# The beginning of a diffusion-layer kernel: more single-tile blocks, products ahead of the modulation matvecs, and another order of loads

## The chip, the cores and the metric

The kernel runs on one core of a Trainium2 chip. The time is the device time of one execution in microseconds; lower is better. Before the change three runs took 2594.56, 2595.95 and 2599.84 us, so the median is 2595.95 us. The execution that was profiled took 2596.07 us.

The engines are named as the profile names them: PE (matrix products; PEld its weight loads), DVE (vector), ACT (scalar and activation), POOL, and SP, which here only issues DMAs. Each engine runs its own instructions in the order of the program and waits on semaphores for the others.

## The reference, cut to what matters

One layer of a hybrid backbone. Only its first step is touched by the change: the modulation vectors of the first FFN, and the beginning of that FFN's first product.

```python
silu_c = jax.nn.silu(c)                  # latent tokens; silu_cc for context tokens
mod_l = (silu_c @ w_mod[l] + b_mod[l]).reshape(B, N_MOD, D_MODEL)    # w_mod: 2048 x 9*2048

def adaln(x, g, mod, i):
    return rms_norm(x, g) * (1 + mod[:, i + 1, None, :]) + mod[:, i, None, :]

def half_step_ffn(x, mod, i, g, w_up, w_down):
    h = adaln(x, g, mod, i)
    a, b = jnp.split(h @ w_up, 2, axis=-1)
    return x + 0.5 * mod[:, i + 2, None, :] * ((jax.nn.silu(a) * b) @ w_down)
```

There are 256 context and 256 latent tokens, the model width is 2048, and all inputs are float32.

## The kernel before, in words

**What the beginning does.** The 2048 columns of the model are 16 tiles of 128 (k = 0 to 15). For each tile k the kernel needs the modulation's shift (i = 0) and scale (i = 1) of these 128 columns for both conditions, before it can form h for that tile; and it can multiply the tile's h by the weights as soon as that is there. So it does not compute all the modulation first. It goes through the columns in `BLOCKS`: two blocks of one tile, (0, 1) and (1, 2), then seven blocks of two tiles.

**One block.** `mod_sums` multiplies the conditions by a 2048 x (block's columns) piece of `w_mod`: 16 small matrix products (32 rows out) per 1 MB load. These are called matvecs here, and the loads are numbered 0 to 31 in the order in which SP issues them (tile `mraw`, four buffers). `mod_turned` copies nothing but turns the sums' rows into columns (PE transposes of `row`) and DVE adds them up to SH (shift) and SC (scale). Then PE turns the tile's columns of x (transposes of `xs`), ACT and DVE form h from them, as a high part `hhi` and a low part `hlo` (`affine_split`: two ACT passes for `hhi`, one pass on ACT and one on DVE for h, one on DVE for `hlo`, for each 256 tokens of a two-tile block).

A block of one tile takes two loads, one for the shift and one for the scale, both by PE. A block of two tiles takes four loads: the first holds the shift of the block's first tile and is summed by DVE in two long passes over 128 x 2048 (`scalar_tensor_tensor`, one for each condition, `junkv<-mraw,cB`); the other three are matvecs of PE. So load 4 was DVE's in block (2, 4), load 8 in (4, 6), load 12 in (6, 8).

**Products.** `products` loads the weights of the first six output units for a block (`w_pre1`, tile `raw`: 384 KB for one tile, 768 KB for two), splits them into `hi` (ACT) and `lo` (DVE), and multiplies: per unit and tile hi by hhi, lo by hhi, and hi by hlo, 128 x 512 each, into six PSUM banks that stay open for all 16 tiles. It is a generator: one step issues the load, the next the split, each further step one unit's products. While a block's matvecs run, PE is given the products of the block before: after each matvec `3 - (k1 - k0)` units, the rest around the block's transposes.

**What sets the order.** Nearly everything in the beginning is pinned: PE, DVE, ACT and SP run it in the order of the Python code. SP issues each load when its buffer has been read by whoever read it last, and in turn: a load that waits holds back all behind it. The four `mraw` buffers go round, so a load of the next block waits for PE's matvec or for DVE's second long pass over a load of this block. After the beginning (about 130 us) comes the rest of the layer, whose code is untouched.

Of the kernel before, what the change touches and what calls it, by code (L numbers as in the profile page):

```python
# [9 lines left out]
F32 = mybir.dt.float32  # L10
F32R = mybir.dt.float32r
BF16 = mybir.dt.bfloat16
FP8 = mybir.dt.float8e5
AF = mybir.ActivationFunctionType
ALU = mybir.AluOpType
# [15 lines left out]

WAIT = 3

N_IDLE = 6, 4, 5, 2, 3

N_HID = 3

# [4 lines left out]

BLOCKS2 = tuple((k, k + 4) for k in range(0, 16, 4))

BLOCKS = ((0, 1), (1, 2)) + tuple((k, k + 2) for k in range(2, 16, 2))
FB = 4
CB = 512
NCB = D // CB
# [10 lines left out]
def tile_layer(ctx: ExitStack, tc: tile.TileContext, I: dict, out: bass.AP):  # L59
# [16 lines left out]
    def tbank():  # L76
        return ps["tr"].tile([P, 512], F32, tag="tr", name="tr")
# [189 lines left out]
    class Beside:  # L267
# [139 lines left out]
    def products(n_ffn, pre, k0, k1, hhi, hlo, early=False, both=False, middle=False):  # L407

        n = (k1 - k0) * P
        most = min(2 * NPRE, 2048 // n // 2 * 2)

        def load(u0):
            nu = min(most, 2 * NPRE - u0)
            raw = raw_tile(n * nu)

            o = (2 * NPRE * k0 * P + u0 * n) * P  # L420
            tc.keep_in_program_order(nc.sync.dma_start(raw, I[f"w_pre{n_ffn}"][o : o + n * nu * P].rearrange("(p c) -> p c", p=P)))
            return raw, nu

        ahead = [load(0)]
        if early:
            wt = split(ahead[0][0], n * ahead[0][1])
        if both:
            ahead.append(load(most))
        yield
        if middle:  # L430
            wt = split(ahead[0][0], n * ahead[0][1])
            early = True
            yield
        for u0 in range(0, 2 * NPRE, most):
            raw, nu = ahead.pop(0)
            if u0 or not early:
                wt = split(raw, n * nu)
            if u0 + most < 2 * NPRE and not ahead:
                ahead.append(load(u0 + most))
            for u in range(nu):  # L440
                b = pre[(u0 + u) // 2][u % 2]
                ws = [(k, wt(slice(u * n + (k - k0) * P, u * n + (k - k0 + 1) * P))) for k in range(k0, k1)]

                for k, (wh, wl) in ws:
                    tensor[0].matmul(b, wh, hhi[:, k, :], start=k == 0, stop=False)  # L445
                    tensor[0].matmul(b, wl, hhi[:, k, :], start=False, stop=False)  # L446
                for k, (wh, wl) in ws:
                    tensor[0].matmul(b, wh, hlo[:, k, :], start=False, stop=k == KT - 1)  # L448
                yield

    xsrc = {CTX: I["ctx"], LAT: I["x"]}
# [10 lines left out]
    with pool(name="st", bufs=1) as st:  # L462
        scratch.append(st)
        cP = st.tile([P, KT, 32], F32, name="cP")
        nc.gpsimd.memset(cP, 0.0)
        pc = tbank()
        nc.tensor.transpose(pc[:, :32], cc, ident[:32, :32])
        nc.vector.tensor_copy(cP[:, :, 0:2], pc[:, :32].rearrange("p (s k) -> p k s", s=2))
# [4 lines left out]

        cB = st.tile([P, 2, D], F32, name="cB")
        junk = st.tile([P, 1024], BF16, name="junkv")
        sel = st.tile([96, P], BF16, name="sel")[:, :32]
        with nc.allow_low_precision("each sum has one term that is not zero, and that is one"):
            vector[0].tensor_reduce(sel, ident[:96, :96].rearrange("p (j q) -> p q j", j=3), axis=AX.X, op=ALU.add)
        c3 = tbank()[:96, :P]
        stack = st.tile([32, P], F32, name="stack")  # L480
        vector[0].tensor_copy(stack[:, :96].rearrange("p (j q) -> p j q", j=3), ident[:32, :32].unsqueeze(1).to_broadcast([32, 3, 32]))
        tensor[0].matmul(c3, stack[:, :96], cc, start=True, stop=True)
        thirds = st.tile([96, P], BF16, name="thirds")
        middle = st.tile([96, P], BF16, name="middle")
# [68 lines left out]
        def mod_unit():  # L553
            if ready:
                return ready.pop(0)
            raw = st.tile([P, 2048], F32, tag="mraw", name="mraw", bufs=4)
            tc.keep_in_program_order(nc.sync.dma_start(raw, I["w_m0"][next(unit)]))
            return raw

        def mod_sums(i, k0, k1, last=iter(())):  # L560

            n = (k1 - k0) * P
            nk = 2048 // n
            b = tbank()[:, :n]
            for g in range(KT // nk):
                if g == KT // nk - 1:
                    steps(last)
                raw = mod_unit()
                for j in range(nk):
                    k = nk * g + j  # L570
                    q = 32 * (j % 4)
                    tensor[0].matmul(
                        b[q : q + 32, :], cP[:, k, :], raw[:, j * n : (j + 1) * n], start=k < 4, stop=k >= KT - 4, tile_position=(0, q), skip_group_check=True
                    )
                yield
            row = st.tile([P, 256], F32, tag="row", name="row", bufs=3)[:, :n]
            scalar[0].activation(row, b, AF.Copy)
            turns.append((i, k0, k1, row))
# [28 lines left out]
        def idle(n):  # L607

            for _ in range(n):
                tensor[0].matmul(pre[2][0][:, :P], ident, ident, start=True, stop=True, skip_group_check=True)  # L610
# [23 lines left out]
        others(1, True)  # L634
        drain(mod_sums(1, 0, 1))
        mod_turned()
        for s in (CTX, LAT):
            scale_of(0, s, slice(0, 1))
        steps(prods)
# [9 lines left out]
        for k0, k1 in BLOCKS[1:]:  # L649
            kk = slice(k0, k1)  # L650
            following = products(1, pre, k0, k1, hhi, hlo, middle=True)
            if k1 - k0 == 2:
                raw = mod_unit()
            for i in range(2):
                for _ in mod_sums(i, k0 if i else k1 - 1, k1, following if i else iter(())):
                    steps(prods, 3 - (k1 - k0))
                if not i and k1 - k0 == 2:
                    for s in (CTX, LAT):
                        vector[0].scalar_tensor_tensor(
                            junk.bitcast(FP8), raw, 1.0, cB[:, s, :], op0=ALU.mult, op1=ALU.mult, accum_out=SH[:, 0, s, k0 : k0 + 1], saturate=False  # L660
                        )
                    biased(0, k0, k0 + 1)

            if k0 != 2:
                steps(following)
            mod_turned()
            if k0 != 2:
                steps(prods)
            for s in (CTX, LAT):
                scale_of(0, s, kk)  # L670
            if k0 == 2:
                steps(following)
                steps(prods)
            if k1 - k0 == 1:
                tb = tbank()
                for s in (CTX, LAT):
                    for t in range(2):
                        x_turned(k0, s, t, tb)
                x_scaled(k0, tb)
            else:  # L680
                for s in (CTX, LAT):
                    drain(to_hT([xs0[s, 0], xs0[s, 1]], 0, s, hhi, hlo, 256 * s, range(k0, k1)))
            drain(prods)
            prods = following
            if k0 == 2:
                scalar[0] = nc.scalar
            if k1 == KT:
                nc.sync.dma_start(ccd.rearrange("s (k p) -> (s k) p", p=P), cc)
# [1770 lines left out]
```

## Time and profile before

| what | value |
|---|---|
| median of three runs | 2595.95 us |
| profiled execution | 2596.07 us, its span 2594.4 us |
| PE busy | 2565.9 us, 99% of the span |
| DVE, ACT, POOL busy | 2183.9, 1432.4, 220.5 us |
| PE busy in the first 130 us | 116.3 us |
| DMA in the first 130 us | 374 GB/s, engines 94% busy |

Where the profile's page counts PE as busy, a row of the timeline gives start, duration, engine, line of the source, operation, the names out<-in, the count, and in brackets the idle time before and what ended it. All pinned instructions of the beginning carry the line of one helper, L87 in the kernel before and L90 in the changed one, so the names tell them apart. A matvec of 16 is counted there as 32 (two passes each).

### The profile page before, as it was taken

Reading aid. Unit: us, or ns where it says so; the run is one execution under the profiler, and the core shown is the slowest. Engines: PE = TensorE matmul, PEld = TensorE weight load, DVE = VectorE, ACT = ScalarE, POOL = GpSimd, SP = SyncE. Lnnn points to the kernel's source line nnn. Section 1 sums busy time; section 2 is a strip of 40 time slices with the busy share of each in tenths; the row PEclk is TensorE's granted clock in tenths of the full one; section 3 lists DMA queues with packets and bytes.
Section 4 is the critical chain, followed back from the end, with each engine's and each line's share of the span. In section 5 each row is a group of like instructions: output and inputs, shape, how many; then the busy total and the mean of one; then the engine's idle time right before and its main releaser. Section 6 shows DMA issues by size and latency. Waiting matters only on the chain. (4 is left out here: it accounts for less than half of the span.)

```text
span 2594.4 us, 34281 instructions
## 1 busy us (share of the span) xinstructions
PE 2565.9 (99%) x12708; PEld 2141.1 (83%) x12708; DVE 2183.9 (84%) x2884; ACT 1432.4 (55%) x1838; POOL 220.5 (8%) x273
## 2 busy tenths in 40 slices
PE   7999999999999999999999999999999999999998
PEld 5788888888888888888889989888898888888887
DVE  6788888878888788888887899798889888888987
ACT  4454444544445565444454448456486676667764
POOL 0000000100000100000110000120000000001001
PEclk9999999999999999999999999999999999999999
DMA  9989999999999989889987897776768999999986
GB/s 396 353 215 266 267 287 273 259 275 287 257 291 264 279 245 244 213 220 224 230 255 258 294 328 239 239 282 212 261 229 251 274 275 277 283 280 284 272 247 174
DMA packets 127656, 684.73 MB, mean 264 GB/s; under 512 B 14200, under 2 KB 16760, under 8 KB 64896
## 3 DMA queue, kind: packets, MB, share of 16 engines
q1 hardware_dynamic: 98112, 490.63, 50.6%
q0 software_dynamic: 29376, 191.90, 37.5%
q8 instruction: 100, 1.64, 0.2%
q14 instruction: 68, 0.56, 0.1%
HBM read 664.59 MB, written 17.89 MB: 263 GB/s over the span
## 5 line engine op out<-in xcount | busy, mean ns | idle before, releaser
L128 ACT ACTIVATE hi<-raw 128x1024 fp32r<-128x1024 f32 (+2 forms) x488 | 505.6, 1040 | 412.6 <-PE mm L152 304.4
L129 DVE TENSOR_TENSOR lo<-raw,hi 128x1024 fp32r<-128x1024 f32 (+2 forms) x476 | 569.0, 1204 | 134.0 <-ACT hi L128 113.2
L128 ACT ACTIVATE hi<-chain 128x1024 fp32r<-128x1024 f32 x352 | 371.9, 1060 | 305.9 <-PE mm L152 184.4
L129 DVE TENSOR_TENSOR lo<-chain,hi 128x1024 fp32r<-128x1024 f32 x352 | 426.5, 1221 | 105.8 <-ACT hi L128 98.3
L152 PE MATMUL mm<-hi,hhi 128*128 128x512 f32 (+3 forms) x1024 | 394.0, 385 | 0.0
L152 PE MATMUL mm<-lo,hhi 128*128 128x512 f32 (+3 forms) x1024 | 386.9, 378 | 0.0
L152 PE MATMUL mm<-hi,hlo 128*128 128x512 f32 (+3 forms) x1024 | 386.4, 377 | 0.0
L208 DVE SCALAR_TENSOR_TENSOR junk<-sraw,cBh 128x1024 fp8e5<-128x1024 f32 x192 | 234.3, 1220 | 21.4 <-DMA sraw<-in_w_mt 19.0
L152 PEld LDWEIGHTS mm<-lo,hhi 128*128 128x128 f32 x1024 | 192.5, 188 | 33.8
L152 PEld LDWEIGHTS mm<-hi,hhi 128*128 128x128 f32 x1024 | 192.6, 188 | 31.1
L152 PEld LDWEIGHTS mm<-hi,hlo 128*128 128x128 f32 x1024 | 192.8, 188 | 30.7
L129 DVE TENSOR_TENSOR lo<-ra,hi 128x1024 fp32r<-128x1024 f32 x104 | 126.3, 1221 | 27.4 <-ACT hi L128 21.6
L128 ACT ACTIVATE hi<-ra 128x1024 fp32r<-128x1024 f32 x104 | 110.2, 1062 | 66.4 <-PE mm L152 40.5
L152 PE MATMUL mm<-lo,hid2h 128*128 128x512 f32 (+1 forms) x356 | 137.9, 387 | 0.1
L152 PE MATMUL mm<-hi,hid2h 128*128 128x512 f32 (+1 forms) x356 | 137.8, 387 | 0.0
L152 PE MATMUL mm<-hi,hid2l 128*128 128x512 f32 (+1 forms) x356 | 137.7, 387 | 0.0
L152 PE MATMUL mm<-hi,sumshl 128*128 128x512 f32 x400 | 123.2, 389 | 0.0
L730 POOL DMA_DIRECT2D chain<-in_w_up1b x60 | 53.1, 886 | 733.5 <-DVE lo L129 733.5
L208 DVE SCALAR_TENSOR_TENSOR sr<-sr,cBl 128x1024 f32<-128x1024 f32 x84 | 102.2, 1224 | 13.4 <-DMA sr<-in_w_mt 7.4
L152 PE MATMUL mm<-hi,sumshh 128*128 128x512 f32 x352 | 108.4, 389 | 0.0
L152 PE MATMUL mm<-hhi,hi 128*128 128x512 f32 (+1 forms) x288 | 101.3, 352 | 0.0
L152 PE MATMUL mm<-hhi,lo 128*128 128x512 f32 (+1 forms) x288 | 99.0, 344 | 0.0
(505 smaller groups left out, 5446.4 us busy)
## 6 DMA issues: line engine op xcount, KB each, us to landing
raw<-in_w_dn SPq DMA_DIRECT2D x70, 1024.0 KB, 9.7
chain<-in_w_up1b POOLq DMA_DIRECT2D x60, 1024.0 KB, 10.6
sraw<-in_w_mt SPq DMA_DIRECT2D x96, 512.0 KB, 8.1
sr<-in_w_mt SPq DMA_DIRECT2D x81, 512.0 KB, 5.6
raw<-in_w_up1b SPq DMA_DIRECT2D x40, 1024.0 KB, 8.0
mraw<-in_w_m SPq DMA_DIRECT2D x32, 1024.0 KB, 8.0
chain<-in_w_dn POOLq DMA_DIRECT2D x30, 1024.0 KB, 9.2
chain<-in_w_up2b POOLq DMA_DIRECT2D x28, 1024.0 KB, 11.2
```

The source lines that it names most:

```text
L128: scalar[0].activation(hi, src, AF.Copy)
L129: vector[0].tensor_tensor(lo, src, hi.bitcast(F32), op=ALU.subtract)
L152: tensor[0].matmul(out_ap, s, m, start=first and not n, stop=last and n == 2, skip_group_check=skip)
L208: ins = nc.vector.scalar_tensor_tensor(junk() if junk else raw, raw, 1.0, cB[s], op0=ALU.mult, op1=ALU.mult, accum_out=mT[:, i, s, kt, h : ...
L730: accum = lambda dst, src: nc.gpsimd.dma_start(dst, src, accum_op=ALU.add)
```

## The change

Five edits, all in the beginning:

- Tiles 2 and 3 become blocks of one tile each (`ALONE = 4`). Loads 4 to 7 are now all summed by PE; DVE's first long passes are those of load 8.
- `AHEAD` says for blocks 1 to 4 how many units of the products of the block before stand ahead of the first matvec and behind each matvec; `idle(N_IDLE[5])` adds four 128 x 128 products that nobody reads behind tile 0's transposes.
- In blocks of one tile the low part's product of a unit stands behind the next unit's high parts ("one unit on").
- Up to block (4, 6) the load of a block's weights is issued behind its last modulation load, where it was issued ahead of it.
- `stack` and `sel`, two small constants, are made by DVE ahead of the copy of the turned conditions.

From block (6, 8) on, and through the whole rest of the layer, every engine has the same instructions in the same order as before, but for the buffers.

PE, from the transposes of tile 0's sums to the first products. Before (`tr<-mraw,cP` is a matvec, `mm<-hhi,hi`, `mm<-hhi,lo` and `mm<-hlo,hi` are a unit's three products):

```order
L87 MATMUL tr<-ident,row 128x128 x2
L87 MATMUL tr<-mraw,cP 32x128 x16
L87 MATMUL mm<-hhi,hi 128x512
L87 MATMUL mm<-hhi,lo 128x512
L87 MATMUL mm<-hlo,hi 128x512
L87 MATMUL mm<-hhi,hi 128x512
```

And now:

```order
L90 MATMUL tr<-ident,row 128x128 x2
L90 MATMUL mm<-ident 128x128 x4
L90 MATMUL mm<-hhi,hi 128x512
L90 MATMUL mm<-hhi,lo 128x512
L90 MATMUL mm<-hhi,hi 128x512
L90 MATMUL mm<-hhi,lo 128x512
L90 MATMUL mm<-hlo,hi 128x512
L90 MATMUL tr<-mraw,cP 32x128 x16
```

The matvec of load 2 has moved behind four idle products and five products of tile 0, and the first product with hlo stands fifth instead of third.

DVE, from tile 1's hlo to the first long passes. Before:

```order
L87 TENSOR_SCALAR h<-tr,SC,SH 128x256
L87 TENSOR_TENSOR hlo<-h,hhi 128x512
L87 SCALAR_TENSOR_TENSOR junkv,SH<-mraw,cB 128x2048 x2
L87 TENSOR_TENSOR SH<-SH,vecs 128x2
L87 TENSOR_REDUCE SH<-tr 128x2
```

And now, where tile 3's hlo is the one ahead of them:

```order
L90 TENSOR_SCALAR h<-tr,SC,SH 128x256
L90 TENSOR_TENSOR hlo<-h,hhi 128x512
L90 SCALAR_TENSOR_TENSOR junkv,SH<-mraw,cB 128x2048 x2
L90 TENSOR_TENSOR SH<-SH,vecs 128x2
L90 TENSOR_REDUCE SH<-tr 128x2
```

The long passes over load 4 are gone, and those over load 8 are the first; they stand behind tile 3's h and hlo (before: behind those of the block of tiles 2 and 3).

SP, the loads 8 to 15, with the engines whose semaphores each waits for (the number in a name only counts the tiles; DMAHW is an earlier load of SP). Before, the rows are loads 9, 10, weights, 11, 12, 13, 14, weights, 15:

```order
L557 DMA mraw_536<-in_w_m0 128x2048 [waits DMAHW6_49,DMAHW2_49,PE_49]
L557 DMA mraw_566<-in_w_m0 128x2048 [waits DMAHW4_49,DVE_49]
L421 DMA raw_582<-in_w_pre1 128x1536 [waits Activation_49]
L557 DMA mraw_584<-in_w_m0 128x2048 [waits DMAHW0_49,PE_49]
L557 DMA mraw_661<-in_w_m0 128x2048 [waits DMAHW2_49,PE_49]
L557 DMA mraw_664<-in_w_m0 128x2048 [waits DMAHW7_49,DMAHW3_49,PE_49]
L557 DMA mraw_694<-in_w_m0 128x2048 [waits DMAHW1_49,DVE_49]
L421 DMA raw_710<-in_w_pre1 128x1536 [waits Activation_49]
L557 DMA mraw_712<-in_w_m0 128x2048 [waits DMAHW5_49,PE_49]
```

And now loads 9, 10, 11, weights, 12, 13, 14, weights, 15:

```order
L563 DMA mraw_614<-in_w_m0 128x2048 [waits DMAHW5_49,DMAHW3_49,PE_49]
L563 DMA mraw_644<-in_w_m0 128x2048 [waits DMAHW7_49,PE_49]
L563 DMA mraw_660<-in_w_m0 128x2048 [waits DMAHW0_49,PE_49]
L424 DMA raw_662<-in_w_pre1 128x1536 [waits DMAHW6_49,DVE_49]
L563 DMA mraw_719<-in_w_m0 128x2048 [waits DMAHW3_49,PE_49]
L563 DMA mraw_722<-in_w_m0 128x2048 [waits DMAHW2_49,DVE_49]
L563 DMA mraw_752<-in_w_m0 128x2048 [waits DMAHW4_49,DMAHW1_49,PE_49]
L424 DMA raw_768<-in_w_pre1 128x1536 [waits Activation_49]
L563 DMA mraw_770<-in_w_m0 128x2048 [waits DMAHW5_49,PE_49]
```

The load that waits for DVE (for the second long pass over load 8) was load 14 and is now load 13, and load 13 is the one whose matvec PE reaches first in block (6, 8).

```diff
-N_IDLE = 6, 4, 5, 2, 3
+N_IDLE = 6, 4, 5, 2, 3, 4
+
+AHEAD = {1: (2, 2, 1), 2: (0, 1, 2), 3: (0, 1, 2), 4: (1, 2, 2, 1)}
...
-BLOCKS = ((0, 1), (1, 2)) + tuple((k, k + 2) for k in range(2, 16, 2))
+ALONE = 4
+BLOCKS = tuple((k, k + 1) for k in range(ALONE)) + tuple((k, k + 2) for k in range(ALONE, 16, 2))
...
+            behind = []
             for u in range(nu):
...
-                for k, (wh, wl) in ws:
-                    tensor[0].matmul(b, wh, hlo[:, k, :], start=False, stop=k == KT - 1)
+                behind += [(b, k, wh) for k, (wh, wl) in ws]
+                while behind and (k1 - k0 > 1 or u == nu - 1 or len(behind) > 1):
+                    o, k, wh = behind.pop(0)
+                    tensor[0].matmul(o, wh, hlo[:, k, :], start=False, stop=k == KT - 1)
                 yield
...
-                if g == KT // nk - 1:
+                if g == KT // nk - 1 and k1 > ALONE + 2:
                     steps(last)
                 raw = mod_unit()
+                if g == KT // nk - 1 and k1 <= ALONE + 2:
+                    steps(last)
...
         mod_turned()
+        idle(N_IDLE[5])
...
+            ahead = iter(AHEAD.get(k0, ()))
+            steps(prods, next(ahead, 0))
             for i in range(2):
                 for _ in mod_sums(i, k0 if i else k1 - 1, k1, following if i else iter(())):
-                    steps(prods, 3 - (k1 - k0))
+                    steps(prods, next(ahead, 3 - (k1 - k0)))
...
-            if k0 != 2:
+            if k0 != ALONE:
                 steps(following)
             mod_turned()
-            if k0 != 2:
+            if k0 != ALONE:
                 steps(prods)
             for s in (CTX, LAT):
                 scale_of(0, s, kk)
-            if k0 == 2:
+            if k0 == ALONE:
                 steps(following)
                 steps(prods)
```

More of the change, by code (lines that the diff above doesn't have):

```diff
@@ L465, in tile_layer @@
         nc.gpsimd.memset(cP, 0.0)
+        stack = st.tile([32, P], F32, name="stack")
+        pin(nc.vector.tensor_copy(stack[:, :96].rearrange("p (j q) -> p j q", j=3), ident[:32, :32].unsqueeze(1).to_broadcast([32, 3, 32])))
+        sel = st.tile([96, P], BF16, name="sel")[:, :32]
+        with nc.allow_low_precision("each sum has one term that is not zero, and that is one"):
+            pin(nc.vector.tensor_reduce(sel, ident[:96, :96].rearrange("p (j q) -> p q j", j=3), axis=AX.X, op=ALU.add))
         pc = tbank()
@@ L475, in tile_layer @@
         junk = st.tile([P, 1024], BF16, name="junkv")
-        sel = st.tile([96, P], BF16, name="sel")[:, :32]
-        with nc.allow_low_precision("each sum has one term that is not zero, and that is one"):
-            vector[0].tensor_reduce(sel, ident[:96, :96].rearrange("p (j q) -> p q j", j=3), axis=AX.X, op=ALU.add)
         c3 = tbank()[:96, :P]
-        stack = st.tile([32, P], F32, name="stack")
-        vector[0].tensor_copy(stack[:, :96].rearrange("p (j q) -> p j q", j=3), ident[:32, :32].unsqueeze(1).to_broadcast([32, 3, 32]))
         tensor[0].matmul(c3, stack[:, :96], cc, start=True, stop=True)
@@ L684, in tile_layer @@
             prods = following
-            if k0 == 2:
+            if k0 == ALONE:
                 scalar[0] = nc.scalar
```

## The prediction

> **What bounds the kernel now.** I read the page's busy shares first, then the stretches of the beginning, then PE's timeline there with the waits in brackets, then the other engines and SP's loads at those waits.
>
> ```profile
> span 2594.4 us, 34281 instructions
> PE 2565.9 (99%) x12708; PEld 2141.1 (83%) x12708; DVE 2183.9 (84%) x2884; ACT 1432.4 (55%) x1838; POOL 220.5 (8%) x273
> ```
>
> PE is the bound. The stretches (length, then busy time of PE, PEld, DVE, ACT, POOL, then the granted clock, DMA share and GB/s) tell where it isn't busy:
>
> ```profile
> 0.00:20.64 20.64, 13.70 (x145) 11.79 (x145) 11.93 (x40) 13.52 (x31) 4.18 (x13) 1.00 0.91 365
> 20.64:58.78 38.14, 31.54 (x292) 21.55 (x293) 24.06 (x51) 16.52 (x33) 0.00 (x0) 0.96 1.01 420
> 58.78:71.93 13.15, 13.15 (x113) 9.29 (x112) 9.70 (x18) 4.98 (x10) 0.00 (x0) 1.00 0.97 369
> 71.93:85.08 13.15, 13.15 (x113) 9.29 (x113) 9.71 (x18) 4.97 (x10) 0.00 (x0) 1.00 0.95 353
> 130.00:2594.40 2464.40, 2449.64 (x11695) 2056.97 (x11693) 2092.77 (x2702) 1373.57 (x1722) 216.27 (x260) 1.00 0.88 258
> ```
>
> From 20.64 (tile 0's sums turned) to 58.78 (first matvec of block (6, 8)) PE idles 38.14 - 31.54 = 6.6 us while the DMA engines are full. From 58.78 on each two-tile block takes PE 13.15 us without a gap. So the end moves by what the arrival in block (6, 8) moves, as long as PE then finds its data; 6.6 us, with the slow clock below about 8, is the most that is there to gain. PE's waits and prices:
>
> ```profile
> 23.61 1.08 PE L87 MATMUL tr<-mraw,cP 128*32 128x128 f32 x32 [2.98 <-DMA mraw<-in_w_m]
> 24.62 0.78 PE L87 MATMUL mm<-hhi,hi 128*128 128x512 f32 x1
> 27.46 1.36 PE L87 MATMUL tr<-mraw,cP 128*32 128x128 f32 x32
> 28.75 0.49 PE L87 MATMUL mm<-hhi,hi 128*128 128x512 f32 x1
> 31.15 0.60 PE L87 MATMUL tr<-ident,xs 128*128 128x128 f32 x4
> 34.63 0.51 PE L87 MATMUL mm<-hlo,hi 128*128 128x512 f32 x1 [0.51 <-DVE hlo L87]
> 38.58 1.07 PE L87 MATMUL tr<-mraw,cP 128*32 128x256 f32 x16 [1.54 <-DMA mraw<-in_w_m]
> 50.83 1.07 PE L87 MATMUL tr<-mraw,cP 128*32 128x256 f32 x16 [1.25 <-DMA mraw<-in_w_m]
> 55.06 1.04 PE L87 MATMUL tr<-ident,xs 128*128 128x128 f32 x8
> 55.86 0.48 PE L87 MATMUL mm<-hhi,hi 128*128 128x512 f32 x1
> 58.78 1.08 PE L87 MATMUL tr<-mraw,cP 128*32 128x128 f32 x32
> 59.79 0.50 PE L87 MATMUL mm<-hhi,hi 128*128 128x512 f32 x1
> 60.13 0.40 PE L87 MATMUL mm<-hhi,lo 128*128 128x512 f32 x1
> 60.36 0.39 PE L87 MATMUL mm<-hhi,hi 128*128 128x512 f32 x1
> 63.98 1.07 PE L87 MATMUL tr<-mraw,cP 128*32 128x256 f32 x16
> ```
>
> Read by starts: a matvec costs 1.01 (58.78 to 59.79), the first product behind it 0.34, each further one 0.23, eight transposes of x 0.80. Matvec and six products after 23.61 run slowly: 24.62 to 27.46 is 2.84 us for 1.5 at these prices, and the matvec of load 3 takes 1.29. That is 1.6 us lost.
>
> **The change, part by part.**
>
> *Products ahead, low part one unit on, idle products.* These fill PE's waits. The first products of tile 0 can start when hhi is there, the first with hlo when DVE has made it:
>
> ```profile
> 21.27 1.02 ACT L87 ACTIVATE hhi<-mm,SH,SC 128x256 fp32r<-128x256 f32 x2 [0.19 <-DVE SC L87]
> 23.36 0.69 DVE L87 TENSOR_TENSOR hlo<-h,hhi 128x512 fp32r<-128x512 f32 x1
> ```
>
> So from 22.3 PE does four products, waits until 24.05 for hlo, then goes on with load 2 (there by 23.61). The four idle products cost nothing: they lie in the wait up to 22.3, and without that cover would cost 0.5. What is late next is hlo, 0.7 us of wait, and at tile 1 the same chain, for which I allow 0.6.
>
> *Two blocks of one tile.* One matvec more on PE (four for tiles 2 and 3 where three were): 1.0 us, on the path. Two turned rows' transposes instead of three per pair become four: 0.1. DVE loses two long passes of 2.3 us and gets a second set of sums. The bytes loaded are the same. Tile 2's products no longer wait for loads 6 and 7, which is what frees PE to run ahead.
>
> *Weights behind the modulation load, earlier constants.* Load 3 comes one 384 KB load sooner (0.9 us at 420 GB/s), its weights one 1 MB load later (2.5 us); their split on ACT stands behind the copy of load 3's sums anyway, so I cost this at nothing, with load 3's matvec as cover; if that cover were gone it would cost up to 2.5. The constants move c's spreading by up to 0.6 us, but x's last load hides all but 0.1 to 0.2 of it.
>
> *The sum up to block (6, 8).* PE's work between 20.64 and 58.78 at full clock is 31.54 - 1.6 = 29.9. With 1.0 + 0.5 + 0.1 more it is 31.5; the waits left are 22.3 - 20.64 less the 0.7 of idle products, 0.7 and 0.6, together 2.2 to 2.3. PE reaches the end of block (4, 6) at 20.64 + 31.5 + 2.2 = 54.3, where before it was 58.78: 4.5 us ahead.
>
> *The wait that is added.* Ahead of that stands load 13. Its buffer is now the one of load 8, which DVE reads twice, and SP holds loads 14, 15 and the block's weights behind it. Before, load 13 waited for a matvec of PE and went out at 48.05; it was load 14 that waited for DVE. The long passes before and SP's loads, each with the time from issue to landing:
>
> ```profile
> 46.12 2.28 DVE L87 SCALAR_TENSOR_TENSOR junkv<-mraw,cB 128x2048 fp8e5<-128x2048 f32 x1
> 48.45 2.29 DVE L87 SCALAR_TENSOR_TENSOR junkv<-mraw,cB 128x2048 fp8e5<-128x2048 f32 x1
> 59.16 0.69 DVE L87 TENSOR_TENSOR hlo<-h,hhi 128x512 fp32r<-128x512 f32 x1
> 48.05 0.33 SPq L557 DMA_DIRECT2D mraw<-in_w_m  x1
> mraw<-in_w_m SPq DMA_DIRECT2D x1, 1024.0 KB, 7.6
> 51.96 0.33 SPq L557 DMA_DIRECT2D mraw<-in_w_m  x1
> mraw<-in_w_m SPq DMA_DIRECT2D x1, 1024.0 KB, 10.4
> 59.92 0.33 SPq L557 DMA_DIRECT2D mraw<-in_w_m  x1
> mraw<-in_w_m SPq DMA_DIRECT2D x1, 1024.0 KB, 6.2
> 73.07 0.33 SPq L557 DMA_DIRECT2D mraw<-in_w_m  x1
> mraw<-in_w_m SPq DMA_DIRECT2D x1, 1024.0 KB, 7.7
> 118.96 0.33 SPq L900 DMA_DIRECT2D raw<-in_w_up1b  x1
> raw<-in_w_up1b SPq DMA_DIRECT2D x1, 1024.0 KB, 4.8
> ```
>
> When do the passes over load 8 end now? Going back from 54.3: tile 3's transposes end ahead of block (4, 6)'s three matvecs (3.0), 18 products (4.2, and 0.5 for first ones), transposes (0.25 and 0.8), and the seven products of tile 2 (1.7), so at about 43.7. In the trace x's transposes for tile 1 began at 31.15 and hlo let the product go at 34.63, so hlo follows the transposes' end by about 2.8: 46.5. Two passes take 4.6 (46.12 to 50.74): load 13 goes out at 51.1, 3 us later than before. At that time only load 12 is ahead of it on the queue, so it does not stand in a stream any more. Its landing is bounded by 4.8 us (118.96, an empty queue) and 7.7 (73.07); I take 6.2, the load at 59.92, which also went out with one load ahead of it. That is 57.3. Load 15 landed 6.7 us behind load 13 before (48.05 + 7.6 and 51.96 + 10.4): now 64.0. Its matvec began at 63.98.
>
> The Trainium skill (DMA: Bandwidth & Descriptors, Anatomy of one DMA) puts a DMA's fixed part at about 2.0 us beside its bytes, which with 1 MB at 436 GB/s is an estimate of 4.4 us: load 13 at 55.5 and load 15 at 62.2. The rows above, 6.2 and 7.7 behind one other load, speak for more.
>
> So the 4.5 us of lead are waited away ahead of loads 13 to 15, and PE goes on from load 15's matvec where it was. With 4.8 instead of 6.2 load 15 lands 1.4 sooner, with 7.7 it lands 1.5 later. I take 6.2, and 0.2 for the earlier constants: the profiled execution's 2596.07 (0.12 above the median) becomes 2595.9.
>
> *The clock.* PE's busy time in three windows of 3.4 us, with the granted clock behind it (the second follows the first):
>
> ```profile
> 21.26:24.68 3.42, 1.07 (x33) 1.00 1.02 424
> 24.68:28.09 3.41, 3.41 (x21) 0.50 1.01 425
> 34.91:38.33 3.42, 2.13 (x20) 1.00 1.02 432
> ```
>
> After a window with 1.07 us of work the clock was halved, after one with 2.13 not. In the changed kernel the first of these holds 0.1 of idle products, 1.0 of products, 0.4 with hlo and 0.3 of matvec: 1.8, nearer to 2.13, so I take full clock. The Trainium skill (TensorE: Matmul & The Clock Gate, What's actually happening) says the clock falls after at least one idle window of about 3.4 us; here a window with 1.07 us of work was enough, so the trace differs. By the page the sum is the same, by the row it may be 1.6 us more.
>
> **Rivals.**
>
> *Load 13 arrives in the stream after all (faster).* If DVE's passes end earlier or the landing takes under 5 us, the next bound is h of tiles 4 and 5: hlo of a two-tile block ended 4.0 us after x's transposes (55.86 to 59.85), so at 58.4, and the unit that began at 59.79 and by the prices was through at 61.3 is through at 58.9. Gain 2.4 at most, 1.4 by the row of 4.8: 2593.7 to 2594.7. For it: the queue is not empty at 51.1. Against it: 59.92 and 73.07. The skill's estimate above, 1.8 us, ends here.
>
> *The lead is kept whole (faster).* 4.5 us: 2591.4. That needs load 13 by 54.3 and hlo by 55, and both rows speak against it.
>
> *The clock falls early (slower).* If 1.8 us of work in the window are too few, PE runs at half clock from 24.68 and everything, tile 3's hlo and load 13 with it, comes 1.6 us later: 2597.5. It decides between 1.07 and 2.13 us.
>
> **How the numbers follow.** The first case (load 15 at about 64) has a chance of 0.52, load 13 in the stream 0.22, the lead kept 0.06, the clock 0.20. Predicted is 2595.9. From 2593.7 to 2597.5 lie all cases but the third; the three runs shown reach 1.4 below and 3.9 above their median, so I give 1.2 on both sides: 2592.5 to 2598.7. About 0.2% (5.2 us) is what a measurement of this kernel can tell from no change. All four cases lie within it; beyond it are only the third with a little scatter, and slow clock with late load and scatter: faster 0.08, the same 0.84, slower 0.08.
>
> **What would show it.** Right: PE's waits between 24 and 54 are gone, PE stands ahead of load 13's matvec for about 3 us, SP issues load 13 when DVE's second pass over load 8 ends near 51, load 15's matvec begins at 63 to 65, and from there blocks of 13.15 us. The clock row shows no half in 24 to 28. Wrong: a matvec of load 15 before 62, or a wait in later blocks ahead of load 17 (which also waits for DVE now) or 19.

## The result, and the profile after

The changed kernel takes 2600.75 us (median of 22 executions, 2596.49 to 2606.44), the kernel before 2596.57 in the same comparison (22, 2594.16 to 2604.02). The ratio is 1.0017, with a 95% interval of 1.0011 to 1.0023: slower, by some 4 us (3.6 by the means, 2600.83 and 2597.20). Forecast were 2595.9 us and a range up to 2598.7.

The profiled execution of the changed kernel took 2596.49 us, which is the lowest of its 22, and that of before 2596.07. So the two traces differ by 0.4 us where the kernels differ by 4: they show the mechanism, but not the size of the loss. Span and busy times after:

```profile
span 2594.8 us, 34441 instructions
PE 2569.3 (99%) x12781; PEld 2143.6 (83%) x12781; DVE 2180.3 (84%) x2887; ACT 1434.1 (55%) x1842; POOL 220.1 (8%) x273
```

The stretches after, with the bounds of the prediction's (length, then busy time of PE, PEld, DVE, ACT, POOL, then granted clock, DMA share, GB/s):

```profile
0.00:20.64 20.64, 14.23 (x147) 12.60 (x148) 12.30 (x40) 13.72 (x31) 3.79 (x13) 1.00 0.90 365
20.64:58.78 38.14, 33.19 (x386) 23.43 (x388) 21.39 (x56) 17.08 (x37) 0.00 (x0) 1.00 0.98 399
58.78:71.93 13.15, 13.15 (x98) 8.82 (x88) 7.62 (x14) 4.31 (x9) 0.00 (x0) 0.87 1.01 417
71.93:85.08 13.15, 13.15 (x113) 9.28 (x111) 9.70 (x17) 5.10 (x11) 0.00 (x0) 1.00 0.95 374
```

In the second stretch PE is busy for 33.19 us instead of 31.54, and idle for 4.95 instead of 6.6; in the third the mean clock is 0.87 (it was full before). PE's timeline at the places of the prediction:

```profile
22.39 0.50 PE L90 MATMUL mm<-hhi,hi 128*128 128x512 f32 x1 [0.82 <-ACT hhi L90]
24.15 0.50 PE L90 MATMUL mm<-hlo,hi 128*128 128x512 f32 x1 [0.57 <-DVE hlo L90]
24.58 1.08 PE L90 MATMUL tr<-mraw,cP 128*32 128x128 f32 x32
58.27 1.08 PE L90 MATMUL tr<-mraw,cP 128*32 128x128 f32 x32 [3.41 <-DMA mraw<-in_w_m]
61.76 1.74 PE L90 MATMUL tr<-mraw,cP 128*32 128x256 f32 x16
65.02 1.07 PE L90 MATMUL tr<-mraw,cP 128*32 128x256 f32 x16
72.93 1.08 PE L90 MATMUL tr<-mraw,cP 128*32 128x128 f32 x32
```

The three waits for loads that the trace of before showed (2.98, 1.54 and 1.25 us) are gone, and one of 3.41 us stands ahead of load 13's matvec (58.27). A small one, 0.45 us at 104.94, comes in a later block. Load 15's matvec begins at 65.02 (before 63.98), block (8, 10) at 72.93 (before 71.93). DVE's second long pass over load 8, and SP's loads 13 and 15 with their times to landing:

```profile
49.08 2.29 DVE L90 SCALAR_TENSOR_TENSOR junkv<-mraw,cB 128x2048 fp8e5<-128x2048 f32 x1
51.40 0.33 SPq L563 DMA_DIRECT2D mraw<-in_w_m  x1
mraw<-in_w_m SPq DMA_DIRECT2D x1, 1024.0 KB, 6.7
52.77 0.65 SPq L563 DMA_DIRECT2D mraw<-in_w_m  x1
mraw<-in_w_m SPq DMA_DIRECT2D x1, 1024.0 KB, 12.1
```

Load 13 goes out when DVE is through (51.40) and lands at 58.1; load 15 lands at 64.9, and PE takes it at 65.02. The first product behind the beginning, before and after:

```profile
133.07 0.39 PE L152 MATMUL mm<-hhi,hi 128*128 128x512 f32 x1
```

```profile
134.54 0.39 PE L155 MATMUL mm<-hhi,hi 128*128 128x512 f32 x1
```

So by these two traces the beginning loses 1.47 us. What comes behind has the same instructions in the same order on every engine. In the profiled execution it gains 1.1 us; by the means of all executions, less this 1.47, it loses some 2.

How much the beginning loses is not the same in every execution. The same two beginnings stand, unchanged, in other profiles. Of the kernels below, c1, c3 and f1 begin as the kernel before, c2, c4 and f2 as the changed one (one profile each, us):

| | load 13 to landing | block (8, 10) begins | first product behind the beginning |
|---|---|---|---|
| before | 7.6 | 71.93 | 133.07 |
| c1 | 7.3 | 71.71 | 133.65 |
| c3 | 5.7 | 72.60 | 133.65 |
| f1 | 8.0 | 72.37 | 133.47 |
| changed | 6.7 | 72.93 | 134.54 |
| c2 | 7.0 | 74.33 | 135.49 |
| c4 | 4.7 | 70.83 | 133.08 |
| f2 | 6.2 | 72.00 | 133.11 |

By the means of four the loss is 0.6 us, and the changed beginning scatters over 2.4 us where that of before scatters over 0.6. When load 13 lands early, something else holds PE. c4's rows of loads 13 and 15:

```profile
mraw<-in_w_m SPq DMA_DIRECT2D x1, 1024.0 KB, 4.7
56.60 1.08 PE L90 MATMUL tr<-mraw,cP 128*32 128x128 f32 x32 [1.84 <-DVE h L90]
62.90 1.07 PE L90 MATMUL tr<-mraw,cP 128*32 128x256 f32 x16 [1.00 <-DMA mraw<-in_w_m]
```

Here load 13 is there at 56.0 (it went out at 51.31), but PE goes on only at 56.60. The matvec's sums take one of two PSUM banks (`tbank`), both of them hold the turned x of tiles 4 and 5, and one comes free when DVE has made the first h. In the kernel before, products of PE covered that time (55.86 to 58.78); now they have been done earlier.

### The profile page after: what moved, and what is told of

Same layout as the page of the kernel before. It is cut to its first block, busy times and chain, and to the rows that moved or that the text cites. A ratio compares the mean times of both kernels' runs of the same rounds, so it can differ in the third digit from the quotient of the medians.

```text
span 2594.8 us, 34441 instructions
## 1 busy us (share of the span) xinstructions
PE 2569.3 (99%) x12781; PEld 2143.6 (83%) x12781; DVE 2180.3 (84%) x2887; ACT 1434.1 (55%) x1842; POOL 220.1 (8%) x273
## 5 line engine op out<-in xcount | busy, mean ns | idle before, releaser
L131 ACT ACTIVATE hi<-raw 128x1024 fp32r<-128x1024 f32 (+3 forms) x486 | 504.2, 1041 | 413.8 <-PE mm L155 308.6
```

Source lines behind the costliest of these rows:

```text
L131: scalar[0].activation(hi, src, AF.Copy)
```

## The experiments

For e, f and g, means and medians are of eleven whole executions, each beside the kernel before in the same comparison (33 executions of it for e1 to e4 and for f1 to f4, 21 for g1 and g2). "By the means" is the difference to that. One execution of these kernels scatters by 1.6 to 3.3 us around its mean (standard deviation), so the mean of eleven is known to some 0.5 to 1 us.

### e1 to e4: the buffer, the clock, the single tiles

e1 lets the four buffers go round as in the kernel before: load 13 takes that of load 10 (a matvec), load 14 that of load 8 (DVE), and so on in the blocks behind; all else of the change stays.

```diff
-            raw = st.tile([P, 2048], F32, tag="mraw", name="mraw", bufs=4)
-            tc.keep_in_program_order(nc.sync.dma_start(raw, I["w_m0"][next(unit)]))
+            n = next(unit)
+            raw = mraws[turn4[n]]
+            tc.keep_in_program_order(nc.sync.dma_start(raw, I["w_m0"][n]))
```

> The changed kernel with one thing undone: the four buffers of the modulation loads go round as in the kernel before, so load 13 waits for PE's matvec of load 10 and load 14 for DVE's second pass over load 8 (in the changed kernel it is the other way round). Theory S (the slot): the 4.4 us of lead with which PE reaches load 13 was lost because load 13 could go out only at 51.4, when DVE gave its buffer back. Then load 13 goes out near 49.7, lands by 56 to 57, PE's wait of 3.4 us ahead of it shrinks to 1.5 to 2, load 15's matvec begins at 62.5 to 63.5 instead of 65.0, and the time is 2594 to 2596, below the kernel before. Theory C (the clock): the same here, since the wait that halves the clock is shorter. Theory R (something in the rest of the layer, not the beginning, is 3 us slower): the beginning gains 1.5 to 2.5, the time stays above the kernel before, near 2598.

Measured: 2600.14 us beside 2597.73, ratio 1.0005 (0.9996 to 1.0014); by the means +1.9. None of the theories gave that time. In its profile load 13 goes out at 49.47 and load 15's matvec begins at 63.66, as theory S said; the time is not what S said.

e2 puts seven products that nobody reads into the wait ahead of load 13.

```diff
             b = tbank()[:, :n]
+            if (i, k0) == (0, ALONE + 3):
+                for _ in range(N_FILL):
+                    tensor[0].matmul(b[:, :P], ident, ident, start=True, stop=True, skip_group_check=True)
```

> The changed kernel with seven idle 128 x 128 products on PE in the wait ahead of load 13's matvec (they add nothing to the sums: the first matvec overwrites them), about 1.5 us of work inside the wait of 3.4 us. Theory S: the loads are as late as ever, so the time is that of the changed kernel, 2600 to 2601. Theory C: the median is above the changed kernel's profiled execution because the halved clock behind the wait costs up to 1.7 us more in executions where the clock's windows lie otherwise; with the wait filled it never falls, and the time is 2598 to 2599. Theory R: unchanged, 2600 to 2601.

Measured: 2598.51, ratio 1.0001 (0.9991 to 1.0011); by the means +1.0. That is theory C's number, but the profile does not show C's gain: the clock stays full and load 14's matvec begins at 61.14 (61.76 in the changed kernel's profile), but PE then waits for load 15.

```profile
65.51 1.07 PE L92 MATMUL tr<-mraw,cP 128*32 128x256 f32 x16 [1.72 <-DMA mraw<-in_w_m]
```

Nor do the products fill the whole wait: they need a bank too, and begin at 56.39, behind a wait of 1.84 us for DVE's h.

e3 is the kernel before with `ALONE = 4` in place of its two single tiles, and nothing else of the change.

> The kernel before with one part of the change alone: tiles 2 and 3 as blocks of their own, without the products ahead, the idle products, the low part one unit on, the other order of loads and constants. In this kernel load 13 waits for PE and load 14 for DVE, as in the kernel before. Theory S: PE keeps its waits up to 30 us (3 us and the slow clock), but reaches block (6, 8) 1 to 3 us sooner and finds load 13 there; the time is 2594 to 2597. Theory R, if it hangs on the two loads more: 2599 to 2600.

Measured: 2601.45, ratio 1.0013 (1.0004 to 1.0021); by the means +3.2, as much as the whole change. Theory S is missed by more than 4 us, theory R by 1.5.

e4 is the change with `ALONE = 2` and `AHEAD = {1: (2, 2, 1)}`: everything but the two more single tiles.

> The changed kernel without the two extra single-tile blocks (tiles 2 and 3 as one block again), with all the rest of the change. Here load 9 and load 13 wait for DVE's passes. Theory S: load 9 goes out near 39 instead of 36.2 and load 13 near 51 instead of 48.05, so load 15's matvec is 1 to 2 us late as in the changed kernel: 2597.5 to 2599. Theory R, if it hangs on the two loads more: 2596 to 2597, as before. What the products ahead and the kept clock win in the first 30 us is waited for again at loads 7 and 11, by either.

Measured: 2597.18, ratio 1.0001 (0.9992 to 1.0010); by the means -0.5, between the two theories' ranges and 0.2 us from R's.

e3 and e4 tell which part it is: the kernels with two more single-tile blocks lose, and without these blocks the products ahead, the low part, the order of loads and the constants are worth nothing that can be measured. e1 and e2 lie between, too close to each other to part the buffer from the clock in whole executions.

### c1 to c8: the beginning by itself

To get rid of the scatter, the kernels were cut off behind the first four output units. c1 is the kernel before, c2 the changed one.

```diff
                 pab.append(b)
-            tail(f, pab)
+            last = tail(f, pab)
+        for t in range(2):
+            for cb in range(NCB):
+                nc.sync.dma_start(out[t * P : (t + 1) * P, cb * CB : (cb + 1) * CB], last)
+    ...
+    return
```

> The kernel before, cut off behind the first four output units of the first product; the last gated unit is written to all of the output, so it does about 165 us of the work and leaves the rest of the layer out. With c2 it says what the beginning alone costs, in many executions instead of one profiled one. Theory B (the beginning as profiled is typical): c2 less c1 is 1.0 to 1.5 us. Theory V (the profiled beginning was a lucky one): c2 less c1 is 3 us or more, all of the loss. Theory W (the loss comes later, where loads and TensorE run neck and neck): c2 less c1 is 1.0 to 1.5 us, and c4 less c3 is 3 us or more.

> The changed kernel, cut off at the same place (about 165 us; the rest of the layer is left out). Against c1: +1.0 to +1.5 us by theories B and W, +3 us or more by V.

c5 to c8 are e1 to e4, cut at the same place.

> e1 (the changed kernel with the four mraw buffers in the order of before, so that load 13 waits for a matvec and load 14 for DVE), cut off behind the beginning as c1 and c2 (the rest of the layer is left out). Theory S (the loss of the beginning comes from load 13 waiting for DVE): at c1's 166.9 or up to 1 us below. Theory C (it comes from the half clock in the wait ahead of load 13): between c1 and c2, as far as the wait is shorter. Theory T (the single tiles' own work and loads): at c2's 168.2.

> e2 (the changed kernel with seven products that nobody reads in the wait ahead of load 13), cut off at the same place. Theory C: 1.3 to 1.6 us below c2, 166.6 to 166.9, with no half clock near 60 us. Theories S and T: at c2's 168.2, since the loads land as late.

> e3 (the kernel before with four single-tile blocks, nothing else of the change), cut off at the same place. If the beginning holds 1.3 us of the single tiles' loss: c1 + 1.3 us, 168.2. If it holds all of it: c1 + 3, about 170.

> e4 (the change with two single-tile blocks as before), cut off at the same place: c1's 166.9, within 0.5 us, if the single tiles carry the loss.

| cut kernel | median us (lowest to highest) | less c1 |
|---|---|---|
| c1 before | 166.87 (165.65 to 167.04) | |
| c2 changed | 168.20 (166.75 to 168.66) | +1.3 |
| c5 changed, buffers in the order of before | 166.17 (165.65 to 167.11) | -0.7 |
| c6 changed, wait filled | 167.58 (167.33 to 167.77) | +0.7 |
| c7 before with four single tiles | 168.83 (168.32 to 169.9) | +2.0 |
| c8 changed, but two single tiles | 166.74 (165.66 to 167.89) | -0.1 |

Four or five executions each, c5 to c8 in another comparison than c1 and c2. One execution scatters by 0.2 to 1.0 us, so a difference of two medians is uncertain by some 0.5. With the buffers in the old order the loss of the beginning is gone, as theory S said. c5's PE row of load 13 and its load:

```profile
56.73 1.94 PE L90 MATMUL tr<-mraw,cP 128*32 128x128 f32 x32 [2.04 <-DMA mraw<-in_w_m]
63.40 1.07 PE L90 MATMUL tr<-mraw,cP 128*32 128x256 f32 x16
```

```profile
49.56 0.33 SPq L570 DMA_DIRECT2D mraw<-in_w_m  x1
mraw<-in_w_m SPq DMA_DIRECT2D x1, 1024.0 KB, 7.0
```

Load 13 goes out 1.84 us sooner than in the changed kernel's profile (49.56 against 51.40) and load 15's matvec begins 1.62 sooner (63.40 against 65.02). e1's profile has nearly the same times, and in both the first product behind the beginning comes at 132.7, earlier than in any profile of the two kernels. The fill of c6 leaves load 13 at 51.30; the 0.6 us of the median is hardly more than the uncertainty. In its profile the clock still fell to half (from 57.78 on), where in e2's it did not, and load 13's matvec stood behind the fill until 58.86 though the load was there at 57.3, so theory C gets no clean test from it. In c7, where the buffers go round as before, single tiles alone cost 2.0. There too DVE's passes stand behind it, by another load: without the products ahead they end at 56.6 in c7's profile and 55.3 in e3's (50.7 before), load 14 goes out only then, and PE waits 0.66 and 0.85 us for load 15. So the rest of the change does pay once the single tiles are there and the buffers go round as before: c5 is 2.7 us below c7.

c3 and c4 are the kernel before and the changed one, cut off behind `for p in range(NP): pair(p)`, with two 1 MB writes of `acc` to the output.

> The kernel before, cut off behind the paired products of the first FFN's second matrix, about 1290 us; the last part of that FFN, the mixers and the second FFN are left out. With c4 it says whether the loss is there by then. Theory B: c4 less c3 is the same 1.0 to 1.5 us as c2 less c1, and the rest of the measured 3 to 4 us comes behind this point or is chance. Theory W: 3 us or more, with waits of TensorE for loads between 160 and 1290 us that the kernel before has less of.

> The changed kernel, cut off at the same place (about 1290 us; the same is left out). Against c3: +1.0 to +1.5 us by theory B, +3 us or more by W and by V.

Measured: 1335.77 (1334.87 to 1340.08, four) and 1340.60 (1338.67 to 1341.98, five). The difference, 4.8 us (3.7 by the means), speaks for W, that most of the loss is there by 1336 us. But in both profiles PE waits near the cut for a load (up to 3.7 us in c3, 6.0 in c4) behind the added writes, which the uncut kernels don't have, so I take the sign from it and not the size.

### f1 to f4: the write at 945 us

c3's profile shows what happens between 935 and 960 us in some executions. SP's third write of the hidden tiles, its time to landing, and the load that stands behind the fourth write; then PE's waits:

```profile
939.16 0.33 SPq L834 DMA_DIRECT2D hid<-stg  x1
hid<-stg SPq DMA_DIRECT2D x1, 256.0 KB, 9.5
951.82 0.33 SPq L1106 DMA_DIRECT2D raw<-in_w_dn  x1
```

```profile
950.59 0.73 PE L152 MATMUL mm<-hi,hidl 128*128 128x512 f32 x2 [0.75 <-ACT hi L128]
951.85 0.50 PE L152 MATMUL mm<-lo,hidl 128*128 128x512 f32 x1 [0.53 <-DVE lo L129]
958.12 0.50 PE L152 MATMUL tr<-lo,hidl 128*128 128x512 f32 x1 [1.89 <-DVE lo L129]
```

The same rows in the profile of the kernel before, where PE does not wait there:

```profile
938.60 0.33 SPq L834 DMA_DIRECT2D hid<-stg  x1
hid<-stg SPq DMA_DIRECT2D x1, 256.0 KB, 5.3
947.10 0.33 SPq L1106 DMA_DIRECT2D raw<-in_w_dn  x1
```

There is one `stg` buffer, so the fourth write cannot be staged until the third has landed, and the load behind it in SP's order waits too. When the third takes 9.5 us instead of 5.3, the load goes out 4.7 later. e1 and e3 show the same in their profiles (8.1 and 8.4 us, and PE waits 1.9 at that place). f1 gives the fourth write a buffer of its own:

```diff
-                stg = chp.tile([P, CB], F32, tag="stg", name="stg")
+                stg = two("late")[:, 0, :] if (n, t) == (NB - 1, 3) else chp.tile([P, CB], F32, tag="stg", name="stg")
```

> The kernel before, in which the last of the four writes of the hidden tiles at 945 us is staged in a buffer of its own, so that it needn't wait until the third has landed (in two of the profiles that wait grew to 8 us and held back a load and, behind it, TensorE by 2.2 to 4.2 us; in the others it cost nothing). Theory W (the loss behind the beginning arises at this place, more often in the changed kernel): f1 is 0.5 to 1 us below before, and f2 only 1.0 to 1.5 us above f1. Theory X (it arises elsewhere): f1 is below before by as much or as little, and f2 is 3 us or more above f1.

> The changed kernel with the same buffer for the last write. Theory W: f2 is 2 to 3 us below the changed kernel's 2600.75, about 2598. Theory X: it stays at 2600 or above.

> The change without the two more single-tile blocks (as e4, which came out at the kernel before within 1 in 1000), with the buffer of f1. By theory W it is 1 to 2 us below before, about 2596; by X at e4's 2597.

f3 asks whether a late start costs more than itself:

```diff
             b = tbank()[:, :n]
+            if (i, k0) == (1, 12):
+                for _ in range(N_LATE):
+                    tensor[0].matmul(b[:, :P], ident, ident, start=True, stop=True, skip_group_check=True)
```

> The kernel before with five 128 x 128 products that nobody reads ahead of a matvec of block (12, 14), 1.3 us of TensorE's time by the fill's 1.83 us for seven, and nothing else changed. It says what it costs the rest of the layer to start later by what c2 less c1 is (1.33 us). Theory N (the rest only moves): before + 1.3 us, about 2599. Theory P (being late there costs more than itself, because loads issued at other moments run into each other): before + 3 us or more.

| kernel | median us | ratio to before (95%) | mean less before's |
|---|---|---|---|
| f1 before, with the buffer | 2594.84 | 0.9995 (0.9986 to 1.0004) | -2.1 |
| f2 changed, with the buffer | 2597.87 | 1.0008 (0.9998 to 1.0017) | +0.7 |
| f3 before, shifted | 2597.60 | 1.0001 (0.9991 to 1.0011) | +0.3 |
| f4 change with two single tiles, with the buffer | 2595.51 | 0.9991 (0.9983 to 1.0000) | -2.0 |

In f1's trace the two writes go out 2.5 us apart (938.68 and 941.17) and the load at 946.90, whatever they take to land. The buffer takes about as much off the kernel before (2.1) as off the changed one (from 3.6 above before to 0.7), and the scatter of one execution (its standard deviation) goes from 3.3 (2.4 to 2.7 in the other comparisons) to 2.0 us. f2's 2597.87 is the number that theory W gave for it; but W also had f1 only 0.5 to 1 below before and f2 1.0 to 1.5 above f1. So this wait is real, but it seems to cost both kernels alike; f2 stays 2.8 us above f1 by the means (uncertain by 0.9), and theory X is nearer than W. By f3 (+0.3, uncertain by 1, where P gave 3 or more) a later start costs no more than itself: theory P falls.

f1 and f4 lie below both kernels, though none of their intervals alone parts them from the kernel before.

### g1 and g2: one DMA more

Beyond the beginning, the kernels with four single tiles share, beside which buffers and banks are in turn, one thing: SP has one DMA more, so every later one takes the next of SP's eight semaphores.

```diff
+            if k0 in MORE:
+                tc.keep_in_program_order(nc.sync.dma_start(dr.tile([32, P], F32, name=f"more{k0}"), cc))
             following = products(1, pre, k0, k1, hhi, hlo, middle=True)
```

> f1 (the kernel before, with a buffer of its own for the last write at 945 us) with one more small DMA of SP in block (8, 10): 16 KB of cc to a place that nobody reads. All later DMAs of SP take the next semaphore, as in the changed kernel; every engine's order is f1's. Theory Q (the place in the rotation costs the missing 1 to 2 us): 1.5 us above f1, about 2596.5. Theory O (it does not): at f1's 2594.8, within its scatter of 2 us for one run (0.6 for eleven).

> f2 (the changed kernel with that buffer) with seven more such DMAs, one in each block from (2, 3) to (12, 14), so that from the end of the beginning on all of SP's DMAs take the semaphores that they take in the kernel before. The seven cost the beginning up to 0.7 us if each holds up a load by 0.1. Theory Q: about 1.5 us below f2's 2597.9, 2596.4. Theory O: 2597.9 to 2598.6.

Measured: g1 2596.55, ratio 0.9992 (0.9983 to 1.0001), by the means 2.3 below before, as f1. g2 2601.06, ratio 1.0011 (1.0002 to 1.0020), 2.3 above, where f2 was 0.7 above. g1's median is the number that theory Q gave, but the kernel before ran 1.6 us longer here than beside f1, and f1 itself was not run again; against before, g1 stands where f1 stood (-2.3 and -2.1), which speaks for O, with an uncertainty of about 1 us for the 1.5 that part the theories. g2 came out above both theories' numbers, presumably because the seven DMAs cost something of their own, and decides nothing. So Q is unlikely, and not excluded.

## Why the prediction was wrong, point by point

**Filling PE's waits: right.** The first product was put at 22.3 and came at 22.39; the first with hlo at 24.05, came at 24.15. PE was to be through with block (4, 6) at 54.3; it was at 58.27 - 3.41 = 54.86, so the lead was 3.9 us instead of 4.5. (The sum counts the idle products as 0.5 us of work and takes 0.7 off the wait for them; with one number for both it ends 0.2 later, nearer to what came.) But 1.8 us of it could not be kept, however early load 13 came, since the matvec also waits for h (c4, 56.60). The prediction has hlo's end only as a bound in a rival, not this one.

**The wait that is added: right in kind, too small in this execution.** Load 13 was to go out at 51.1 and went out at 51.40. It was to land after 6.2 us, within 4.8 to 7.7; it took 6.7. Load 15 then came 6.7 us later, as said. That puts load 15 at 64.9 instead of 64.0, and its matvec at 65.02 instead of 63.98. One step that failed is the sentence that PE "goes on from load 15's matvec where it was": with 6.2, the middle of the bounds, the sum ended just at the old time, so that 0.3 us more of issue and 0.5 more of landing, which the bounds allowed, make a loss of 1 us. Over the four profiles of this beginning the landing was 6.15 in the mean, so 6.2 was well chosen; what the sum lacked is that a late landing costs its lateness, and an early one wins only a part. In c4 it came 1.5 us sooner than 6.2, and the beginning ended 0.4 us ahead of the mean of those of before. c5 and e1 show that it is this wait: with the old order of buffers the beginning is 2.0 us shorter than c2, and 0.7 shorter than c1. The Trainium skill's fixed 2.0 us (DMA: Bandwidth & Descriptors, Anatomy of one DMA), which that section gives for transfers that POOL issues, makes an estimate of 4.4 for this load of SP; the runs lie on both sides of the rows' 6.2, from 4.7 (c4) to 7.0 (c2, c5), all of them above the estimate.

**The rest of the layer: the larger miss.** This is the step that put the time outside the range: the prediction says that "the end moves by what the arrival in block (6, 8) moves, as long as PE then finds its data", and so puts what comes behind the beginning at nothing. With the beginning's loss alone (1.3 us by the cut kernels, 1.5 by the two traces) the time would lie between 2597 and 2598, inside. The beginning gives 1.3 us (c2 less c1) to 2.0 (c7 less c1). Whole executions with four single tiles lose more:

| pair | whole executions, means | beginning alone | left over |
|---|---|---|---|
| changed, before | +3.6 | +1.3 | 2.3 |
| e3, before | +3.2 | +2.0 | 1.2 |
| e1, before | +1.9 | -0.7 | 2.6 |
| e2, before | +1.0 | +0.7 | 0.3 |
| f2, f1 | +2.8 | +1.3 | 1.5 |

Each row is uncertain by about 1 us, and the rows share c1 and the kernel before; together they leave some 1.6 us, uncertain by about 0.6, where e4 against before leaves -0.4 and f4 against f1 0.3. So a loss behind the beginning is likely, and not more than that. What makes it is open: it is not the later start (f3), the write at 945 us does not explain it (f1, f2), and the rotation of SP's semaphores is unlikely (g1). Which banks and buffers the rest gets in turn was not tried. In single profiles PE's waits in the rest fall in different places each time (at 945 us, near 1500, between 1800 and 1900, behind 2100), so no one trace can tell.

**The clock: right where it was argued, missed where it wasn't.** Early it kept full speed, as said: the two windows there held 2.56 and 2.68 us of work, and the stretch of the prediction, 21.26 to 24.68, 2.04 (1.8 was said). In c2, the same beginning, it did fall early, but at 16.05, ahead of the part that was argued; load 13 then went out at 52.62, 1.2 us later. But the prediction itself put a wait of 3 us ahead of load 13, and did not ask what that does to the clock. PE's busy time and the granted clock in windows of 3.41 us of the changed kernel, two early and three around that wait:

```profile
18.80:22.21 3.41, 2.56 (x42) 2.01 (x42) 1.87 (x9) 3.06 (x6) 0.00 (x0) 1.00 1.04 432
22.21:25.63 3.42, 2.68 (x38) 1.71 (x38) 1.31 (x3) 2.26 (x3) 0.00 (x0) 1.00 1.01 421
...
52.93:56.35 3.42, 1.89 (x14) 1.28 (x12) 2.70 (x9) 3.19 (x7) 0.00 (x0) 1.00 0.92 371
56.35:59.76 3.41, 1.49 (x34) 1.27 (x35) 3.34 (x5) 1.26 (x4) 0.00 (x0) 1.00 1.00 419
59.76:63.17 3.41, 3.41 (x22) 1.64 (x20) 3.38 (x4) 0.76 (x2) 0.00 (x0) 0.50 1.02 429
```

The half clock stretched load 14's matvec from 1.07 to 1.74 us. Of this little came through, since load 15 landed only 0.15 us ahead of its matvec, and in e2, with the clock full, PE waited for load 15 instead.

**The rivals.** None came true in the profiled execution. Load 13 did not come in the stream, the lead was not kept, and the clock did not fall early. In c4's execution the first one did in part: the landing took 4.7, near its row's 4.8, and load 15's matvec began at 62.90, 1.1 us ahead of the old time. The same execution shows one of the prediction's signs of being wrong, a wait of 0.96 us for load 19 (77.05). The case that happened, the added wait a little longer than the lead and a loss behind it, was in no rival; the slower one should have been the landing at its upper bound of 7.7, which by the prediction's own numbers gave +1.5 us.

**The range.** 1.2 us on both sides for scatter came from three executions; the kernel before scatters by 2.4 to 3.3. Over all comparisons the kernel before alone ran from 2590.70 to 2607.16 us, and its median from 2596.57 to 2599.33.

## What to carry to other kernels

A lead that ends in a wait for a load is worth what the load's landing allows: find the last reader of the buffer that the next load takes, and when a step changes which load that is, count it with the landing at its upper bound. Ask also what else the engine waits for at that place: here products that used to cover a wait of 1.8 us for a bank had been moved away. A change of 1 us in a kernel that scatters by 3 is measured by cutting the kernel off behind the changed part, where the scatter here was 0.2 to 1.0; one profiled execution may be the luckiest of its kind. A single staging buffer between a write and the next one puts the write's landing on the path of everything behind it in that queue.

## What the runs showed of the hardware that was not expected

In these traces PE's clock changes in steps of 3.41 us: half clock lasted 3.41 us in the beginning of each kernel in which it came (6.83 in c7), and the full clock ahead of it 13.65 us in the kernel before, 27.31 in c3 and 47.79 in the changed kernel, which are 4, 8 and 14 times 3.41. How much work such a window holds goes with what follows it, and the line lies near half of a window. The fullest window seen here that was followed by half clock, in c8, held 1.65 us (its row and the next):

```profile
12.67:16.09 3.42, 1.65 (x13) 1.46 (x14) 2.57 (x12) 2.90 (x8) 1.03 (x2) 1.00 1.02 429
16.09:19.50 3.41, 3.41 (x40) 2.71 (x40) 2.48 (x3) 0.57 (x3) 0.14 (x1) 0.50 1.03 422
```

The changed kernel kept full clock after 1.89 (the row from 52.93 above) and e4 after 2.00. But c4 kept it after 1.62:

```profile
54.81:58.22 3.41, 1.62 (x35) 1.34 (x36) 3.34 (x6) 2.69 (x7) 0.00 (x0) 1.00 0.99 413
58.22:61.64 3.42, 3.42 (x27) 1.91 (x25) 3.38 (x4) 1.25 (x2) 0.00 (x0) 1.00 1.03 434
```

So by PE's busy time, whose ends are modelled, the line is not sharp. The Trainium skill (TensorE: Matmul & The Clock Gate, What's actually happening) says that the window is free-running and does not start with the kernel. The traces agree: the kernel before fell to half at 24.68 us in its profile and at 39.21 in c3, and e4's beginning fell at 16.09 in c8 and not at all in e4. So the same wait can cost up to 1.7 us (an estimate: half of a window of 3.41) in one execution and nothing in another.

A 256 KB write to memory, issued beside a 1 MB load of POOL at the same place of the program, took 5.3 us to land in one execution and 9.5 in another. A 1 MB load (load 13) took 4.7 us in one execution and 7.0 in another, behind the same DMAs of its queue.
